# A Hymba-style layer: the gate's adaLN on ScalarE and GpSimd, the S5 scan emitted without delay, u's chunks first, q and k in place

## The chip, the core and the metric

The kernel runs on one core of a Trainium2 chip. The metric is the time of one execution on the device in microseconds. The engines are TensorE (PE, with its weight loads PEld), VectorE (DVE), ScalarE (ACT), GpSimd (POOL) and SyncE (SP). SP issues the DMAs of all large weights, POOL those of the small inputs and of data that goes through DRAM. Each engine takes its instructions in the order of its own queue.

## What is computed

One decoder layer on 256 tokens of width 4096, all in fp32:

```python
mod = silu(c) @ w_ada + b_ada
shift, scale, gate = split(mod, 3)
h = x * (1.0 + scale) + shift
q, k, v, g_lr, z_gla, u_s5, z_s5 = split(h @ w_in)
o_gla = RMSNorm_head(GLA(q, k, v, alpha(g_lr))) * silu(z_gla)   # 4 heads, chunks of 64
y = gelu(S5(u_s5))                # 128 groups of 16 channels, 64 complex states each
y = y * sigmoid(y @ w_glu + b_glu)
o_s5 = y * silu(z_s5)
mixed = concat(o_gla, o_s5) @ w_out
x = layer_norm(2 ** 0.25 * x + gate * mixed, ln_g, ln_b)
```

`w_ada` is 4096 x 12288, `w_in` 4096 x 10256, `w_out` 4096 x 4096, `w_glu` 2048 x 2048. Every weight is read once.

## The kernel before

**Matmuls.** Each weight tile of 512 KB comes into one of six `raw` buffers (`raw`, L81; the buffers are shared by all weights, in the order of SP's queue). `split` (L109) makes two fp32r halves of it: ACT rounds it to `hi` (L114) and DVE takes the rest as `lo` (L115). PE then multiplies hi by hi, hi by lo and lo by hi: 12 matmuls for a tile (L211 for `w_in`, L733 for `w_out`, L587 for `w_glu`). There are three buffers each for `hi` and `lo`.

**adaLN.** c @ w_ada is a product with one row only, so it is not done on PE: the pieces of `w_ada` come as 128 x 1024 tiles, 32 to a piece, and DVE adds tile times silu(c) to `rows` (`ada_sums`, L143: the first step at L151, the other 31 at L153). PE then sums `rows` over the partitions. Eight pieces make shift and scale, each for one block of 512 of the 4096 inputs of `w_in` (`ada_steps`). Four more make the gate (`gate_steps`, L704), which is needed at the end alone; its bias and its result pass through POOL's DMAs (L713, L717).

**Input projection.** The 21 column chunks of `KINDS` are visited in each of 8 blocks of the inputs (`win_plan`); some visits take two blocks at once. Partial sums are kept in SBUF and added by DVE (L222). In the last block (b = 7) a chunk is finished. A zs chunk is then transposed and sent to DRAM through POOL (L231, L232). A u chunk is transposed and copied by 32 small ACT copies into `u4` (`s5_u4`, L416). From the ninth chunk on, steps of the S5 work are emitted behind each chunk with `later(LATE)`, which puts them 60 priority steps back; behind a zg chunk a GLA head follows (`gla_head`). It writes the decayed q and k into a buffer of its own, `qkt` (L607, L634, L636).

**S5.** `s5_inputs` (L424) makes the input of the states, `e`, in 16 blocks. Two scans (`s5_scan`, L468), one for each half of the groups, run over 64 chunks of four tokens: 63 steps each, four small DVE instructions to a step (L475 to L478), each step needing the one before. `s5_outputs` (L520) makes 16 blocks of outputs: the states (L502) need the finished scan of their half, `s5_lags` copies a Toeplitz block with 16 ACT copies (L518), and PE (L548) and ACT (L555) finish y. The first scan is driven from `s5_inputs` (blocks 8 to 15, L438), the second from `s5_outputs` (L536, L543), both at the lowered priority of the work around them.

**Order of the end.** First half of the output projection (`wout(cc, 0)`, the GLA channels) with `s5_outputs` between its tiles, then GLU, then the second half with the residuals (L754 to L758), then the layer norm. Gate steps are emitted between the weight tiles of all these, so many to a tile as `GATE_RATES` says: for the S5 chunks of the last block, its other chunks, the first half, GLU, the second half. A scheduler then orders every engine's queue by these priorities and by when it expects inputs to be ready.

Of the kernel before, what the change touches and what calls it, by code (L numbers as in the profile page):

```python
# [14 lines left out]
AF = mybir.ActivationFunctionType  # L15
ALU = mybir.AluOpType
PSUM = bass.MemoryType.PSUM

P = 128
D = 4096  # L20
SEQ = 256
# [4 lines left out]
DK_SCALE = 256 ** -0.5  # L26
# [10 lines left out]
ADA_LEAD = 1  # L37

RATES = (1.3, 0.85)
GATE_RATES = (1.2, 0.2, 0.7, 0.6, 0.6)  # L40

PAIRED = (6, 7, 7, 7, 7, 8, 7)


KINDS = (
    [("zs", i) for i in range(4)]
    + [("u", i) for i in range(4)]
    + [("qk", 0), ("va", 0), ("vb", 0), ("zg", 0)]
    + [c for h in range(1, 4) for c in (("qk", h), ("v", h), ("zg", h))]
)  # L50
# [7 lines left out]
class Emit:  # L58
# [81 lines left out]
        self.gg = load("gg", [P, DV // P], io["gla_norm_g"])  # L140


    def ada_sums(self, piece):  # L143

        nc = self.nc
        self.rows = rows = self.tmp([P, 1024], "rows")
        for kt in range(32):
            t = self.raw([P, 1024], self.io["ada"][piece, kt])
            c = self.silu_c[:, kt : kt + 1]
            if kt == 0:  # L150
                nc.vector.tensor_scalar(out=rows, in0=t, scalar1=c, scalar2=None, op0=ALU.mult)  # L151
            else:
                nc.vector.scalar_tensor_tensor(out=rows, in0=t, scalar=c, in1=rows, op0=ALU.mult, op1=ALU.add)  # L153
            yield
# [269 lines left out]
    def s5_inputs(self):  # L424

        nc = self.nc
        flat = "p k g h -> p (k g h)"

        e = self.bp.tile([P, 162, 2, 32], F32, tag="b32", name="e")
        self.e, self.bcols = [e[:, 1:65], e[:, 98:162]], e[:, 65:97]  # L430

        nc.gpsimd.memset(e[:, 0:98:97], 0.0)

        self.moved = [e[:, 0:97], e[:, 65:161]]
        scans = [self.s5_scan(0), self.s5_scan(1)]
        self.scans = scans
        nb = NPAIR // NB
        scan = lambda b, n: drive(scans[0], n) if b >= 8 else None  # L438
        loads = {b: self.s5_load(self.io["s5_b"][b]) for b in range(2)}
        prep = lambda b: self.pad_products(self.pad[b % 2], loads.pop(b), self.pw[:, :, :, b * NB : (b + 1) * NB], 1, True)  # L440
        prep(0)
        for b in range(nb):
            pad, w1s = self.pad[b % 2], []
            for n2 in range(NB // 2):
                tps = self.zbank([P, 2, 2, P])
                for m in range(2):
                    for ri in range(2):
                        nc.tensor.transpose(out=tps[:, m, ri], in_=pad[:, 2 * n2 + m, ri].rearrange(flat), identity=self.ident)
                w1s.append(self.tmp([P, 2, 2, P], "w1"))
                nc.scalar.copy(out=w1s[-1], in_=tps)  # L450
                if n2 == 0 and b + 1 < nb:
                    prep(b + 1)
                    if b + 2 < nb:
                        loads[b + 2] = self.s5_load(self.io["s5_b"][b + 2])
                scan(b, 3)
                yield
            eps = self.zbank([P, 2, 64, NB])
            for n in range(NB):
                pr = b * NB + n
# [60 lines left out]
    def s5_outputs(self):  # L520


        nc = self.nc
        nb = NPAIR // NB
        self.y = []
        self.ct_next = None
        self.dd = [self.cp.tile([P, NB, 32], F32, name=f"dd{i}") for i in range(2)]
        for t in self.dd:
            nc.gpsimd.memset(t, 0.0)
        self.s5_prep(0)  # L530
        yield
        nxt = None
        for b in range(-1, nb):
            ys = nxt
            if b < 7:
                drive(self.scans[1], 4)  # L536
            if b + 1 < nb:
                kt, nxt = self.s5_states(b + 1)
            if b + 2 < nb:
                self.s5_prep(b + 2)  # L540
            yield
            if b < 7:
                drive(self.scans[1], 4)  # L543
            if b >= 0:
                o = self.zbank([P, NB, 64])
                for n in range(NB):
                    pr = b * NB + n
                    nc.tensor.matmul(o[:, n], lhsT=self.w0[b % 2][:, n], rhs=self.u4[pr // 16][:, pr % 16, :], start=True, stop=True)  # L548
                nc.vector.tensor_tensor(out=o, in0=o, in1=ys, op=ALU.add)
                if b % 4 == 0:  # L550
                    self.y.append(self.slot([P, 4, SEQ], name="y"))
                yv = self.y[-1][:, b % 4].rearrange("p (j c) -> p j c", j=4)
                for a in range(NB):
                    for j in range(4):
                        nc.scalar.activation(out=yv[32 * a : 32 * a + 32, j], in_=o[32 * j : 32 * j + 32, a], func=AF.Gelu_apprx_tanh)  # L555
# [48 lines left out]
    def gla_head(self, h):  # L604
        nc = self.nc
        v = nc.vector
        qk = self.slot([P, 2, 2, SEQ], name="qkt")  # L607
        q, k = qk[:, 0], qk[:, 1]

        ps = self.xbank([P, 2, SEQ])  # L610
        wg = self.tmp([16, 2, P], "wg")
# [19 lines left out]
                            in1=lv[:, :, c - 1, CH - 1 : CH].broadcast_to([P, 2, c]), op=ALU.add)  # L631
        nc.scalar.activation(out=ds_, in_=ds_, func=AF.Exp, scale=1.0 / TAU)
        nc.scalar.activation(out=x, in_=l, func=AF.Exp, scale=1.0 / TAU)
        v.scalar_tensor_tensor(out=q, in0=self.turned(self.acc["qk"][h], 0), scalar=DK_SCALE, in1=x, op0=ALU.mult, op1=ALU.mult)  # L634
        nc.scalar.activation(out=x, in_=l, func=AF.Exp, scale=-1.0 / TAU)
        v.tensor_tensor(out=k, in0=self.turned(self.acc["qk"][h], 2), in1=x, op=ALU.mult)  # L636

        ap = self.xbank([P, 3, P])
        kv = k.rearrange("p t (c n) -> p t c n", n=CH)
# [33 lines left out]
        o = zg  # L673
# [30 lines left out]
    def gate_steps(self):  # L704

        nc, io = self.nc, self.io
        self.gates = []
        for qd in range(4):
            yield from self.ada_sums(8 + qd)
            gate = self.dp.tile([1, 1024], F32, tag=f"gate{qd}", name=f"gate{qd}")  # L710
            for j in range(2):
                b = self.tmp([1, 512], "gb")
                nc.gpsimd.dma_start(out=b, in_=io["b_ada_g"][:, qd * 1024 + j * 512 : qd * 1024 + j * 512 + 512])  # L713
                ps = self.xbank()
                nc.tensor.matmul(ps[0:1], lhsT=self.ones[:, 0:1], rhs=self.rows[:, 512 * j : 512 * j + 512], start=True, stop=True)
                nc.vector.tensor_tensor(out=b, in0=ps[0:1], in1=b, op=ALU.add)
                nc.gpsimd.dma_start(out=gate[:, 512 * j : 512 * j + 512], in_=b)  # L717
            self.gates.append(gate)
# [274 lines left out]
```

## Time and profile before

| | us |
|---|---|
| median of 3 runs | 1730.19 (1728.96 to 1730.79) |
| the profiled execution | 1725.37 |
| its span, first to last instruction | 1723.6 |
| mean granted clock of TensorE | 0.959 |

The profile is one execution on the hardware. The lines quoted below come from it: busy times, windows cut from the span, waits with what ended them, and groups of instructions as "line engine operation, output <- inputs, shapes, count | busy us, mean ns of one | idle us before it". A granted clock of 1.00 is full speed.

### The profile page before, as it was taken

To read this page: it belongs to the slowest core of one execution; us is meant where nothing else is said; L and a number is where in the kernel's file an instruction comes from. 1 tells how busy PE (TensorE), PEld (TensorE's weight loads), DVE (VectorE), ACT (ScalarE), POOL (GpSimd) and SP (SyncE) were. 2 spreads that over 40 slices of the span, in tenths; PEclk is the share of its full clock that TensorE was granted. 3 is DMA by queue.
4 is the path that set the end of the run, shared out by engine and by line. 5 is a ranking of instruction groups with operands and counts; after the bars stand their busy time and mean duration, and the time that the engine had idled before them with its cause. 6 is when DMAs were issued, how large, how long until landed. Compare 5 with 4: busy or idle time off the path is not lost. (4 is left out here: it accounts for less than half of the span.)

```text
span 1723.6 us, 22261 instructions
## 1 busy us (share of the span) xinstructions
PE 1540.7 (89%) x7548; PEld 1282.8 (74%) x7548; DVE 1457.9 (85%) x2096; ACT 830.2 (48%) x1468; POOL 67.2 (4%) x134
## 2 busy tenths in 40 slices
PE   0689999999999999998988999869973989999995
PEld 0577888888888888877777888657763879977773
DVE  7899889898998999988966699978897468979986
ACT  0345434343343433533587777538732975533330
POOL 1000000000000000000000000000000000010000
PEclk9999999999999999999999999978995999999997
DMA  9999999999999999989965546316890279989982
GB/s 363 348 358 347 352 337 346 337 346 352 334 347 341 338 356 336 339 303 323 325 227 200 166 146 204 118 40 188 300 339 16 74 254 312 332 305 359 337 301 109
DMA packets 138066, 480.64 MB, mean 279 GB/s; under 512 B 17899, under 2 KB 18363, under 8 KB 137691
## 3 DMA queue, kind: packets, MB, share of 16 engines
q1 hardware_dynamic: 130240, 457.85, 74.1%
q0 software_dynamic: 7712, 21.37, 3.9%
q8 instruction: 59, 0.97, 0.2%
q14 instruction: 55, 0.45, 0.1%
HBM read 472.77 MB, written 6.39 MB: 278 GB/s over the span
## 5 line engine op out<-in xcount | busy, mean ns | idle before, releaser
L114 ACT CAST hi<-raw 128x1024 fp32r<-128x1024 f32 (+2 forms) x496 | 506.5, 1025 | 647.3 <-DMA raw<-in_w_in 207.6
L115 DVE TENSOR_TENSOR lo<-raw,hi 128x1024 fp32r<-128x1024 f32 (+2 forms) x496 | 583.4, 1186 | 115.1 <-ACT hi L114 110.5
L211 PE MATMUL mm<-hi,hhi 128*128 128x512 f32 (+2 forms) x1344 | 514.0, 386 | 28.3 <-ACT hi L114 22.1
L211 PE MATMUL mm<-hi,hlo 128*128 128x512 f32 (+2 forms) x1344 | 511.2, 383 | 0.0
L153 DVE SCALAR_TENSOR_TENSOR rows<-raw,silu_c,rows 128x1024 f32<-128x1024 f32 x372 | 476.3, 1280 | 32.2 <-DMA raw<-in_ada 28.9
L211 PE MATMUL mm<-lo,hhi 128*128 128x512 f32 (+2 forms) x1344 | 351.6, 383 | 2.6 <-DVE lo L115 2.5
L211 PEld LDWEIGHTS mm<-hi,hhi 128*128 128x128 f32 x1344 | 254.5, 189 | 81.5 <-ACT hi L114 26.4
L211 PEld LDWEIGHTS mm<-hi,hlo 128*128 128x128 f32 x1344 | 254.8, 190 | 48.0 <-issue 0.2
L211 PEld LDWEIGHTS mm<-lo,hhi 128*128 128x128 f32 x1344 | 245.7, 189 | 51.6 <-DVE lo L115 4.9
L733 PE MATMUL mm<-hi,ohi 128*128 128x512 f32 x512 | 205.2, 402 | 5.1 <-ACT hi L114 5.1
L733 PE MATMUL mm<-hi,olo 128*128 128x512 f32 x512 | 203.2, 397 | 0.6 <-DVE olo L683 0.5
L733 PE MATMUL mm<-lo,ohi 128*128 128x512 f32 x512 | 143.6, 400 | 4.1 <-DVE lo L115 4.0
L733 PEld LDWEIGHTS mm<-hi,ohi 128*128 128x128 f32 x512 | 97.8, 191 | 30.9 <-ACT hi L114 7.9
L733 PEld LDWEIGHTS mm<-lo,ohi 128*128 128x128 f32 x512 | 95.1, 190 | 29.4 <-DVE lo L115 8.7
L733 PEld LDWEIGHTS mm<-hi,olo 128*128 128x128 f32 x512 | 97.8, 191 | 21.6 <-DVE olo L683 1.6
L502 PE MATMUL pz<-e,pad 128*128 128x97 f32 (+1 forms) x256 | 51.6, 369 | 41.9 <-DVE e L478 41.9
L502 PEld LDWEIGHTS pz<-e,pad 128*128 128x128 f32 x256 | 48.5, 257 | 45.4 <-DVE e L478 42.7
L587 PE MATMUL mm<-yhl,hi 128*128 128x256 f32 x512 | 68.5, 288 | 5.0 <-ACT hi L114 5.0
L587 PEld LDWEIGHTS mm<-yhl,hi 128*128 128x128 f32 x512 | 65.4, 196 | 5.3 <-ACT hi L114 5.2
L166 PE MATMUL px<-ones,rows 128*128 128x1 f32 x128 | 16.5, 258 | 53.5 <-DVE rows L153 53.5
L518 ACT COPY w<-px 32x128 f32<-32x128 f32 (+3 forms) x256 | 55.5, 217 | 11.3 <-PE px L515 7.0
L166 PEld LDWEIGHTS px<-ones,rows 128*128 128x128 f32 x128 | 17.2, 209 | 54.2 <-DVE rows L153 53.5
(238 smaller groups left out, 1199.1 us busy)
## 6 DMA issues: line engine op xcount, KB each, us to landing
raw<-in_ada SPq DMA_DIRECT2D x384, 512.0 KB, 5.6
raw<-in_w_in SPq DMA_DIRECT2D x304, 512.0 KB, 5.3
raw<-in_w_out SPq DMA_DIRECT2D x128, 512.0 KB, 5.1
raw<-in_w_glu SPq DMA_DIRECT2D x32, 512.0 KB, 4.9
raw<-in_w_vb SPq DMA_DIRECT2D x16, 272.0 KB, 3.8
x<-in_xT POOLq DMA_DIRECT2D x16, 256.0 KB, 5.0
raw<-in_w_va SPq DMA_DIRECT2D x16, 256.0 KB, 4.3
xo<-in_x_tok POOLq DMA_DIRECT2D x8, 512.0 KB, 6.9
```

The source lines that it names most:

```text
L114: nc.scalar.copy(out=hi, in_=src)
L115: nc.vector.tensor_tensor(out=lo, in0=src, in1=hi.bitcast(F32), op=ALU.subtract)
L153: nc.vector.scalar_tensor_tensor(out=rows, in0=t, scalar=c, in1=rows, op0=ALU.mult, op1=ALU.add)
L166: nc.tensor.matmul(ps[:, s, kt : kt + 1], lhsT=self.rows[:, 512 * s + kt * P : 512 * s + kt * P + P], rhs=self.ones[:, 0:1], start=True, s ...
L211: nc.tensor.matmul(ps[:, m, 0:w], lhsT=t[:, 2 * half + kt, m * P : m * P + P], rhs=r[:, kt], start=st, stop=en)
L502: nc.tensor.matmul(yps[:, n, 0 : moved.shape[1]], lhsT=pad[:, n, ri].rearrange("p k g h -> p (k g h)"), rhs=moved[:, :, ri, (b * NB + n) % ...
L518: nc.scalar.copy(out=w0[32 * j : 32 * j + 32, n, 32 * j : P], in_=kps[32 * n : 32 * n + 32, 0 : P - 32 * j])
L587: nc.tensor.matmul(ps[:, m], lhsT=w[:, kt, m * P : m * P + P], rhs=t[:, kt, :], start=u == 0 and j == 0, stop=u == 3 and j == len(todo) - 1)
L733: nc.tensor.matmul(ps[:, it], lhsT=t[:, 2 * n2 + m, it * P : it * P + P], rhs=w[:, m], start=first and j in (0, 2), stop=last and j >= len ...
```

## The change

- `ada_sums` gets a form `aside`, used for the gate's four pieces: ACT multiplies a tile by silu(c) in place (the first one into `rows`), and POOL adds it to `rows`. DVE has no part in it. A tile's buffer is now free when POOL has read it.
- `GATE_RATES` is 0.85 throughout.
- The scans are emitted with the delay taken back (`later(-LATE)`, `later(-BG_LATE)`), and the second one in sixes.
- In `KINDS` u's four chunks stand ahead of zs's.
- `gla_head` writes q and k into the buffer of their own projection sums, `acc["qk"][h]`, and makes both transposes before the first write.

```diff
-GATE_RATES = (1.2, 0.2, 0.7, 0.6, 0.6)
+GATE_RATES = (0.85, 0.85, 0.85, 0.85, 0.85)
...
-    [("zs", i) for i in range(4)]
-    + [("u", i) for i in range(4)]
+    [("u", i) for i in range(4)]
+    + [("zs", i) for i in range(4)]
...
+            if aside:
+                o = t if kt else rows
+                nc.scalar.activation(out=o, in_=t, func=AF.Copy, scale=c)
+                if kt:
+                    nc.gpsimd.tensor_tensor(out=rows, in0=t, in1=rows, op=ALU.add)
+            elif kt == 0:
...
-        scan = lambda b, n: drive(scans[0], n) if b >= 8 else None
+        def scan(b, n):
+            with self.later(-LATE):
+                drive(scans[0], n if b >= 8 else 0)
...
-            if b < 7:
-                drive(self.scans[1], 4)
+            with self.later(-BG_LATE):
+                drive(self.scans[1], 6)
...
-        qk = self.slot([P, 2, 2, SEQ], name="qkt")
-        q, k = qk[:, 0], qk[:, 1]
+        qk = self.acc["qk"][h]
+        q, k = (qk[:, t].rearrange("p (t n) -> p t n", t=2) for t in range(2))
...
+        tq, tk = (self.turned(qk, t) for t in (0, 2))
...
-            yield from self.ada_sums(8 + qd)
+            yield from self.ada_sums(8 + qd, True)
```

The lines of the changed kernel are up to 10 higher than those of the kernel before: L743 is L733 there, L511 is L502, L557 is L548, L484 to L487 are L475 to L478, L514 is L505; the gate's products are L152, its sums L154.

**PE, ninth block of states.** PE's queue in the first half of the output projection, where it first needs the second scan (`e`); before:

```order
L733 MATMUL mm_11202<-hi_11448,olo_9262 128x512
L733 MATMUL mm_11202<-lo_11449,ohi_9261 128x512 x4
L502 MATMUL pz_10787<-e,pad_391 128x96 x8
L548 MATMUL pz_10827<-u_1339_6912,w_1_394 128x64 x4
L515 MATMUL px_10870<-ident,kt_10796 128x128
L502 MATMUL pz_10912<-e,pad_392 128x96 x8
L515 MATMUL px_11017<-ident,kt_10921 128x128
```

and in the changed kernel:

```order
L743 MATMUL mm_11045<-hi_11239,olo_8606 128x512
L743 MATMUL mm_11045<-lo_11240,ohi_8605 128x512 x4
L511 MATMUL pz_10933<-e,pad_391 128x96 x8
L557 MATMUL pz_10977<-u_1285_6666,w_1_394 128x64 x4
L743 MATMUL mm_11045<-hi_11283,ohi_9371 128x512
```

Before, 576 of the 768 matmuls of this half stand ahead of the ninth block, 280 of them since the eighth, and three blocks follow one another; now 456 stand ahead, 108 since the eighth, and matmuls of the projection stand between the blocks.

**DVE, the second scan.** Two of its late steps on DVE, before (`rows` is the gate's sum):

```order
L115 TENSOR_TENSOR lo_11575<-raw_11572,hi_11574 128x1024
L477 TENSOR_TENSOR sc_1993_9872<-sc_1993_9872,e 128x64
L153 SCALAR_TENSOR_TENSOR rows_9747<-raw_11610,silu_c,rows_9747 128x1024
L478 TENSOR_TENSOR e<-sc_1993_9872,sc_1994_9873 128x64
L475 TENSOR_TENSOR sc_1995_9878<-a_307,e 128x64
L476 TENSOR_TENSOR sc_1996_9879<-a_307,e 128x64
L477 TENSOR_TENSOR sc_1995_9878<-sc_1995_9878,e 128x64
L153 SCALAR_TENSOR_TENSOR rows_9747<-raw_11653,silu_c,rows_9747 128x1024
L478 TENSOR_TENSOR e<-sc_1995_9878,sc_1996_9879 128x64
```

and the scan's last two steps now, with the first use of its result (`kt`):

```order
L115 TENSOR_TENSOR lo_11240<-raw_11237,hi_11239 128x1024
L486 TENSOR_TENSOR sc_2129_10483<-sc_2129_10483,e 128x64
L487 TENSOR_TENSOR e<-sc_2129_10483,sc_2130_10484 128x64
L484 TENSOR_TENSOR sc_2131_10489<-a_307,e 128x64
L485 TENSOR_TENSOR sc_2132_10490<-a_307,e 128x64
L486 TENSOR_TENSOR sc_2131_10489<-sc_2131_10489,e 128x64
L487 TENSOR_TENSOR e<-sc_2131_10489,sc_2132_10490 128x64
L115 TENSOR_TENSOR lo_11284<-raw_11281,hi_11283 128x1024
L514 TENSOR_TENSOR kt_10942<-pz_10933,dd_9440 128x128
```

The gate's steps no longer stand among the scan's. Counted in this stage's splits (L115), the second scan ends behind 51 of them before and behind 38 now; between the ends of the two scans stood 31 gate steps.

**ACT and POOL in GLU.** ACT's queue in GLU before:

```order
L114 CAST hi_12432<-raw_12430 128x1024
L114 CAST hi_12465<-raw_12463 128x1024
L114 CAST hi_12495<-raw_12493 128x1024
L592 ACTIVATE sg_12421<-mm_12291,bglu 128x256 x2
L114 CAST hi_12528<-raw_12526 128x1024
L600 CAST ohi_12425<-sg_12421 128x2x4x64
```

and now (L601 and L609 are L592 and L600):

```order
L152 ACTIVATE raw_12453<-raw_12453,silu_c 128x1024
L114 CAST hi_12459<-raw_12457 128x1024
L152 ACTIVATE raw_12487<-raw_12487,silu_c 128x1024
L114 CAST hi_12503<-raw_12501 128x1024
L601 ACTIVATE sg_12491<-mm_12354,bglu 128x256 x2
L114 CAST hi_12533<-raw_12531 128x1024
L609 CAST ohi_12350<-sg_12491 128x2x4x64
L152 ACTIVATE raw_12561<-raw_12561,silu_c 128x1024
```

A product now stands ahead of most splits. POOL's queue has seldom more than DMA issues before; in GLU it now reads:

```order
L587 DMA zsq_12498<-zsd 128x1024
L154 TENSOR_TENSOR rows_12129<-raw_12419,rows_12129 128x1024
L154 TENSOR_TENSOR rows_12129<-raw_12453,rows_12129 128x1024
L154 TENSOR_TENSOR rows_12129<-raw_12487,rows_12129 128x1024
L154 TENSOR_TENSOR rows_12129<-raw_12561,rows_12129 128x1024
```

Each sum waits for its product and for the sum before it, and SP's load into the buffer waits for the sum. Of the gate's 128 loads in SP's queue, 26 stood in the last block of the input projection, 45 in the first half of the output projection, 19 in GLU and 38 in the second half; now it is 45, 55, 26 and 2.

More of the change, by code (lines that the diff above doesn't have):

```diff
@@ L140, in consts, with ada_sums @@
         self.gg = load("gg", [P, DV // P], io["gla_norm_g"])
-    def ada_sums(self, piece):
+    def ada_sums(self, piece, aside=False):
         nc = self.nc
@@ L149, in ada_sums @@
             c = self.silu_c[:, kt : kt + 1]
-            if kt == 0:
+            if aside:
[4 more added lines that the diff above has]
+            elif kt == 0:
                 nc.vector.tensor_scalar(out=rows, in0=t, scalar1=c, scalar2=None, op0=ALU.mult)
@@ L541, in s5_outputs @@
             yield
-            if b < 7:
-                drive(self.scans[1], 4)
+            with self.later(-BG_LATE):
+                drive(self.scans[1], 6)
             if b >= 0:
@@ L633, in gla_head @@
         nc.scalar.activation(out=x, in_=l, func=AF.Exp, scale=1.0 / TAU)
-        v.scalar_tensor_tensor(out=q, in0=self.turned(self.acc["qk"][h], 0), scalar=DK_SCALE, in1=x, op0=ALU.mult, op1=ALU.mult)
+        tq, tk = (self.turned(qk, t) for t in (0, 2))
+        v.scalar_tensor_tensor(out=q, in0=tq, scalar=DK_SCALE, in1=x, op0=ALU.mult, op1=ALU.mult)
         nc.scalar.activation(out=x, in_=l, func=AF.Exp, scale=-1.0 / TAU)
-        v.tensor_tensor(out=k, in0=self.turned(self.acc["qk"][h], 2), in1=x, op=ALU.mult)
+        v.tensor_tensor(out=k, in0=tk, in1=x, op=ALU.mult)
         ap = self.xbank([P, 3, P])
```

## The prediction

> **What bounds the kernel now.** I read the page's busy shares first, then cut the span into six stages with the windows view, and then asked which waits of TensorE (PE) end last in each stage.
>
> ```profile
> PE 1540.7 (89%) x7548; PEld 1282.8 (74%) x7548; DVE 1457.9 (85%) x2096; ACT 830.2 (48%) x1468; POOL 67.2 (4%) x134
> ```
>
> PE is nearest to full, DVE next, and POOL is almost empty. These are averages. The windows below are P0 (everything up to the last block of the input projection), C (that last block), W0 (first half of the output projection, with the S5 outputs), G (GLU), W1 (second half of the output projection) and the tail T.
>
> ```profile
> 0.00:838.00 838.00, 758.47 (x3511) 631.72 (x3512) 746.59 (x817) 333.77 (x377) 17.86 (x38) 1.00 0.94 341
> 838.00:1075.00 237.00, 226.42 (x1228) 188.88 (x1228) 185.75 (x327) 172.71 (x331) 15.91 (x34) 0.98 0.61 205
> 1075.00:1409.50 334.50, 267.42 (x1246) 219.42 (x1245) 259.31 (x692) 200.86 (x615) 14.28 (x28) 0.86 0.47 158
> 1409.50:1509.90 100.40, 95.36 (x775) 94.91 (x774) 86.76 (x76) 56.32 (x82) 2.65 (x5) 0.97 0.92 330
> 1509.90:1695.00 185.10, 181.11 (x776) 143.33 (x774) 160.12 (x147) 66.16 (x65) 16.50 (x30) 1.00 0.84 303
> 1695.00:1723.60 28.60, 11.96 (x18) 4.56 (x18) 19.33 (x42) 0.36 (x1) 0.00 (x0) 0.55 0.39 147
> ```
>
> Columns: length, then busy time of PE, PE's weight loads, DVE, ACT, POOL, then granted clock, DMA share, GB/s. W1, C and G keep PE at 95 to 98%. P0's loss is mostly one wait of 53.5 us at its start. W0 is the poor stage: 267.4 of 334.5 us, at a clock of 0.86. PE's waits there (us, times, longest), behind that one of P0:
>
> ```profile
> PE px L166 <- DVE rows L153: 53.5, 1, 53.5
> ...
> PE pz L502 <- DVE e L478: 41.9, 2, 34.4
> PE pz L548 <- ACT y L555: 7.0, 3, 3.3
> PE pz L548 <- ACT w L518: 4.9, 8, 1.5
> ```
>
> Two waits make 41.9 us: the S5 states (L502) stand in PE's queue behind the last step of a scan on DVE (L478). Each also costs clock. Four windows of 20 us around them, same columns:
>
> ```profile
> 1140.00:1160.00 20.00, 12.42 (x49) 9.79 (x50) 15.52 (x65) 7.15 (x32) 1.57 (x3) 0.63 0.09 32
> 1160.00:1180.00 20.00, 17.37 (x75) 13.64 (x75) 15.36 (x29) 17.38 (x63) 2.63 (x5) 0.76 0.47 139
> 1300.00:1320.00 20.00, 1.82 (x8) 1.83 (x9) 17.29 (x96) 0.00 (x0) 0.00 (x0) 0.50 0.00 0
> 1320.00:1340.00 20.00, 13.94 (x63) 13.17 (x63) 9.94 (x20) 15.39 (x68) 1.07 (x2) 0.50 0.02 7
> ```
>
> From 1300 to 1320 PE stands and DVE is busy; then PE works 13.94 us at half clock. At full clock those 13.94 would take 7.0, the 12.42 at 0.63 would take 7.8 and the 17.37 at 0.76 would take 13.2: 15.8 us lost, as far as clock scales busy time.
>
> **The change part by part.**
>
> *Scan.* Its 126 steps are the same instructions, only emitted without the delay. The order shows why a wait can go: before, PE asks for the ninth block of states after 576 of W0's 768 matmuls; now after 456, and the scan's end has moved from behind 51 of this stage's splits (L115) to behind 38, which is where PE's 456 matmuls (12 each) stand. Before, 31 of the gate's multiply-adds stood between the two scans' ends too.
>
> ```profile
> L153 DVE SCALAR_TENSOR_TENSOR rows<-raw,silu_c,rows 128x1024 f32<-128x1024 f32 x372 | 476.3, 1280 | 32.2 <-DMA raw<-in_ada 28.9
> L151 DVE TENSOR_SCALAR rows<-raw,silu_c x12: 733/750/755, 10.8 to 1536.3; 128x1024 f32<-128x1024 f32 x12
> ```
>
> 31 times 1.28 is 40 us less in front of the second scan, more than the 34.4 it is late. So I take both waits as gone: 41.9 + 15.8 = 57.7 us gross, and C plus W0 shrink from 571.5 to 513.8. What is late next is below.
>
> *Gate.* DVE loses 124 x 1.280 + 4 x 0.75 = 161.7 us. ACT gains 128 products, POOL 124 sums. The nearest ACT rows:
>
> ```profile
> L114 ACT CAST hi<-raw 128x1024 fp32r<-128x1024 f32 x464 | 486.5, 1052 | 605.0 <-DMA raw<-in_w_in 207.6 <-PE mm L211 161.0 <-DMA raw<-in_w_out 84.6
> L175 ACT ACTIVATE x<-x,m 128x256 f32<-128x256 f32 x32 | 16.6, 591 | 59.0 <-DVE m L170 58.9
> L176 ACT CAST hhi<-x 128x256 fp32r<-128x256 f32 x32 | 10.9, 400 | 0.0
> L416 ACT COPY u<-px 32x128 f32<-32x128 f32 x128 | 32.9, 257 | 3.1 <-PE px L246 1.5
> ```
>
> L175 reads two operands per partition and is 191 ns longer than L176 of the same size; the product reads one, so 1052 + 95 = 1147 ns. By the load order, the gate's loads become 45 in C, 55 in W0, 26 in G, 2 in W1 (26, 45, 19, 38 before). ACT in C and W0 then has 172.71 + 200.86 + 100 x 1.147 = 488.3 us of work, 95% of the 513.8. The densest long stretch that ACT reaches in this trace is 39.43 of 43 us, 92%:
>
> ```profile
> 1333.00:1376.00 43.00, 40.67 (x206) 36.11 (x206) 19.00 (x32) 39.43 (x155) 0.00 (x0) 0.88 0.22 69
> ```
>
> At 91.7% the two stages need 532.5 us. **ACT takes the scan's place as the bound, and 57.7 gross becomes 39.0 net.** PE then runs (226.4 + 267.4 - 15.8) / 532.5 = 90%, and DVE (185.8 + 259.3 less the 71 steps that its loads put there, 91) is at 66%. Behind a product in ACT's queue stand the splits that PE waits for, so this load is on the path.
>
> No row shows a POOL sum. The nearest is a memset of the same tile, one pass over it:
>
> ```profile
> L385 POOL MEMSET pad<- x2: 978/978/978, 3.5 to 4.4; 128x1024 f32 x2
> ```
>
> From below 0.98 us; from above three such passes (two reads, one write), 2.93; I take two, 1.96, as if the write runs beside the reads, and keep both ends. 98 sums in C and W0 are then 192 us (96 to 287) beside 30 of other work in 532: hidden as long as nothing is shared. A sum also holds its load buffer, so the load queue (SP) now waits for POOL, and POOL's own DMA issues (S5 weights, zsd, the next gate's bias) stand between sums. In G one step in 100.4 / 32 = 3.1 us leaves room for 0.85 of a sum at any of the three prices.
>
> The Trainium skill (GPSIMD Engine Reference, Elementwise — side-by-side cycle accounting) gives 4497 ns for an fp32 sum of 2048 elements; half of it, 2.25 us, is an estimate by that page, and no run shown here has such a sum. With it the sum of this part stays as it is.
>
> *G.* Loads rise from 51 to 58 in the order and ACT from 56.3 to 86 of 100.4 us. A DMA share of 0.92 times 58/51 is 1.05, 5 us too much where P0 sustains 0.94, unless some loads land earlier, as W0's share of 0.47 lets them. I cost it at 0 (-2 to +6): its first wait stays ACT's, the first row here:
>
> ```profile
> PE mm L587 <- ACT hi L114: 5.0, 1, 5.0
> PE mm L733 <- DVE lo L115: 2.7, 4, 1.1
> ```
>
> *W1* (second row) loses nearly all gate work, 36 loads and 44.7 us of DVE; PE is at 181.1 of 185.1, so it gains 3 at most; I take 3. *T* has none of it: 0.
>
> *u first.* 32.9 us of ACT copies (L416) move ahead of the zs chunks, but products now stand between them; in C, PE's waits are these:
>
> ```profile
> PE mm L211 <- ACT hi L114: 4.8, 2, 4.4
> PE px L246 <- ACT u L416: 4.5, 3, 2.7
> ```
>
> ACT's total in C is counted above, so I add nothing (-9.3 to +10). *q, k in place* drops four buffers and issues the same instructions; k's transposes must now end before q is written: 0, and at most half of the 4.9 us that they all take. P0 has the same chunk widths: 0.
>
> ```profile
> L246 PE MATMUL px<-ident,qk 128*128 128x128 f32 x32 | 4.9, 274 | 0.0
> ```
>
> **Sum.** The profiled execution took 1725.37 us (span 1723.6 and 1.8 around it); 1725.4 - 39.0 - 3.0 = 1683.4. It lies 4.8 under the median of the three runs, 1730.19, against which the change is timed, so the forecast is 1688.
>
> **The rivals.**
>
> *PE-bound (1656).* ACT packs better than in any long stretch so far, and C and W0 run at C's PE share of 95.5%: 478 / 0.955 = 500.5, 71 saved instead of 39. Against it: the L548 waits on ACT, 11.9 us, exist already with less on ACT.
>
> *POOL and DVE in turn (slower, about 1750).* DVE's instructions with two inputs in SBUF and POOL's sums share something and run one at a time. DVE's work of that kind in G and in C plus W0:
>
> ```profile
> 838.00:1075.00 237.00, 68.55 (x58) 0.98 0.61 205
> 1075.00:1409.50 334.50, 72.29 (x60) 0.86 0.47 158
> 1409.50:1509.90 100.40, 40.80 (x34) 0.97 0.92 330
> L475 DVE TENSOR_TENSOR sc<-a,e 128x64 f32<-128x64 f32 x126 | 28.0, 222 | 2.6
> L477 DVE TENSOR_TENSOR sc<-sc,e 128x64 f32<-128x64 f32 x126 | 27.4, 218 | 0.0
> L396 DVE TENSOR_TENSOR ta<-bc,pw 128x512 f32<-128x512 f32 x32 | 20.8, 685 | 0.0
> L396 DVE TENSOR_TENSOR ta<-bc,af 128x512 f32<-128x512 f32 x32 | 20.5, 677 | 0.0
> L399 DVE TENSOR_TENSOR ta<-ta,ta 128x512 f32<-128x512 f32 x16 | 11.0, 686 | 0.0
> L406 DVE TENSOR_TENSOR pad<-ta,ta 64x512 f32<-64x512 f32 x32 | 21.8, 682 | 1.0 <-PE pz L502 0.7
> L580 DVE TENSOR_TENSOR y<-y,zsq 128x1024 f32<-128x1024 f32 x4 | 8.2, 2043 | 0.0
> L593 DVE TENSOR_TENSOR sg<-y,sg 128x512 f32<-128x512 f32 x8 | 5.5, 685 | 0.0
> L601 DVE TENSOR_TENSOR olo<-sg,ohi 128x512 fp32r<-128x512 f32 x8 | 8.9, 1114 | 0.0
> ```
>
> The first three rows are L115 alone by stage. C plus W0: 140.8 + 4 x 27.7 for the scan + 74.1 = 326; G: 63.4. With a sum of p us, G needs 63.4 + 27p instead of 100.4 and C plus W0 326 + 98p instead of 532.5. Both excesses together eat the 42 us from p = 2.28. At 1.96 this costs 16 in G alone, 1704; at 2.45, midway to the upper end, 29 + 34, which gives 1751; at 2.93, 1811. For it: a scan step is a chain of four such instructions, so its wait would come back. Against it: nothing in this trace, which has no POOL read.
>
> The Trainium skill (SBUF — State Buffer, Who interferes with whom) states this rule: a VectorE instruction with two SBUF inputs and a GpSimd instruction that reads SBUF exclude each other for whole instructions. By it and the 2.25 us above the change would about break even; no run here can show it yet, and the trace neither agrees nor disagrees.
>
> *ACT packs worse (1727).* At 85% busy C and W0 need 574, and only W1's 3 us remain, less G's start.
>
> *The scan's wait half stays (1709).* The change then does only half of what it says: the scan's last steps and PE's request moved up together (38 splits, 456 matmuls), and if DVE's queue is held by the splits' waits for ACT, one of the two waits returns at about half of 42.
>
> **How the numbers follow.** Forecast 0.45, its own range 1670 to 1705; PE-bound 0.13; POOL and DVE in turn 0.27; ACT packs worse 0.08; wait half stays 0.07. From 1652 to 1752 all but the edges of the first rival and the dearer half of the second are in. A measurement of this kernel tells about 0.2%, 3.5 us, from no change. Faster: 0.45 + 0.13 + 0.07 and a little of the second rival, 0.67; within 0.2%: 0.06; slower 0.27.
>
> **What would show it.** PE's wait for L478 gone and the clock of W0 near 0.95: the scan step is right. ACT above 90% through C and W0 with PE waiting for L114 or L518: the bound is right. L115 stretched beyond 1.19 us, or POOL sums stretched where DVE is busy, and G longer than 105 us: the second rival. Sums above 2.3 us would make my forecast wrong even without it, since the load queue waits for them.

## The result and the profile after

| | before | after |
|---|---|---|
| median of the timed runs, us | 1729.58 (1726.97 to 1730.79) | 1839.44 (1834.70 to 1847.42) |
| span of the profiled execution, us | 1723.6 | 1837.2 |
| mean granted clock of TensorE | 0.959 | 0.938 |

The changed kernel is slower: its time is 1.0651 of that before (95% interval 1.0628 to 1.0674), where the forecast said 1688 us and a range up to 1752.

The page after, its row of busy times:

```profile
PE 1598.9 (87%) x7548; PEld 1318.0 (72%) x7548; DVE 1517.1 (83%) x1968; ACT 963.6 (52%) x1596; POOL 398.9 (22%) x258
```

DVE lost 128 gate instructions and yet is busy for 59 us more (1457.9 before). Something stretched those that stayed.

The windows view of the kernel after, by stage. Columns as before: length, busy time of PE, its weight loads, DVE, ACT, POOL, then clock, DMA share, GB/s. C and W0 are taken together, because the edge between them is not sharp in every kernel: from 838 us to the GLU's first matmul.

```profile
0.00:838.00 838.00, 758.75 (x3498) 632.50 (x3498) 740.95 (x807) 336.19 (x378) 22.16 (x39) 0.99 0.93 340
838.00:1497.00 659.00, 545.57 (x2492) 436.23 (x2493) 520.18 (x960) 477.28 (x1050) 270.03 (x155) 0.87 0.53 177
1497.00:1628.70 131.70, 105.80 (x770) 100.98 (x769) 111.71 (x51) 81.89 (x102) 88.06 (x37) 0.92 0.78 271
1628.70:1807.90 179.20, 176.78 (x772) 143.77 (x770) 123.86 (x110) 67.87 (x66) 18.64 (x28) 1.00 0.67 218
```

Cut in the same way, the kernel before has 570.6, 101.3 and 183.9 us in the last three rows. Its row of C and W0:

```profile
838.00:1408.60 570.60, 492.94 (x2465) 407.40 (x2465) 444.15 (x1016) 372.73 (x942) 30.19 (x62) 0.91 0.52 177
```

So C and W0 took 88.4 us more, G 30.4 more, W1 4.7 less: 114.1, against 113.6 between the two spans. DVE is busy for 520 us in C and W0 (444 before) though it has 56 instructions fewer.

The waits of PE in the kernel after (us in total, times, longest):

```profile
PE px L171 <- DVE rows L158: 54.6, 1, 54.6
PE mm L743 <- DVE lo L115: 37.0, 13, 6.1
PE mm L216 <- ACT hi L114: 19.8, 12, 5.4
PE mm L596 <- DVE lo L115: 18.7, 17, 4.0
PE mm L216 <- DVE lo L115: 16.8, 7, 6.7
```

The two waits for the scan, 41.9 us before, are not in the list any more. In their place stand waits for L115, the second half of a split: 37.0 us in W0 and W1 (4.0 before), 18.7 in G (none before) and 16.8 in the input projection (2.5 before). The groups of instructions behind that, in the kernel after (of the first row busy us and mean ns, of the others ns least/median/most):

```profile
L115 DVE TENSOR_TENSOR lo<-raw,hi 128x1024 fp32r<-128x1024 f32 (+2 forms) x496 | 666.8, 1356 | 173.3 <-ACT hi L114 167.9
L487 DVE TENSOR_TENSOR e<-sc,sc x126: 205/224/2535, 1020.5 to 1370.1; 128x64 f32<-128x64 f32 x126
L152 ACT ACTIVATE raw<-raw,silu_c x124: 1131/1149/1185, 830.8 to 1623.2; 128x1024 f32<-128x1024 f32 x124
L154 POOL TENSOR_TENSOR rows<-raw,rows x124: 2342/2467/3622, 832.0 to 1634.0; 128x1024 f32<-128x1024 f32 x124
```

L115 grew from 583.4 to 666.8 us, and the scan's last step, never far from its 0.22 us before, takes up to 2.5. The product on ACT is at the 1.147 us of the forecast; the sum on POOL is at 2.34 to 3.62 instead of 1.96. The timeline of DVE shows what the long steps are:

```profile
1077.51 2.54 DVE L487 TENSOR_TENSOR e<-sc,sc 128x64 f32<-128x64 f32 x1
1080.08 2.38 DVE L484 TENSOR_TENSOR sc<-a,e 128x64 f32<-128x64 f32 x1
1082.38 0.21 DVE L485 TENSOR_TENSOR sc<-a,e 128x64 f32<-128x64 f32 x1
```

and in the same timeline the engine POOL (x2 are two sums behind each other):

```profile
1077.58 4.80 POOL L154 TENSOR_TENSOR rows<-raw,rows 128x1024 f32<-128x1024 f32 x2
```

Two sums run from 1077.58 to 1082.38. Two instructions of the scan, of 0.22 us else, take 2.54 and 2.38 us beside them and end when they end, and the third, at 1082.38, is short again. DVE gets one instruction through for each sum. It is so in the whole trace: all 31 scan instructions that took over 0.32 us end 0.08 to 0.09 us after a sum does, and all 49 splits of 128x1024 over 1.32 us end 1.08 to 1.09 us after one.

### The profile page after: what moved, and what is told of

The parts are those of the page before. It is cut to its first block, busy times and chain, and to the rows that moved or that the text cites. A ratio compares the mean times of both kernels' runs of the same rounds, so it can differ in the third digit from the quotient of the medians.

```text
span 1837.2 us, 22440 instructions
## 1 busy us (share of the span) xinstructions
PE 1598.9 (87%) x7548; PEld 1318.0 (72%) x7548; DVE 1517.1 (83%) x1968; ACT 963.6 (52%) x1596; POOL 398.9 (22%) x258
## 4 chain that ended last, share of the span: by engine, by line
PE 51%; DVE 20%; ACT 14%; issue 7%; DMA 7%; SPq 0%; DVEq 0%; ACTq 0%
PE mm L216 36%; PE mm L743 11%; DVE lo L115 6%; ACT hi L114 3%; DVE rows L158 3%; DMA raw<-in_ada 3%; ACT w L527 2%; ACT y L564 2%; ACT raw L152 2%; DMA raw<-in_w_in 2%; DVE e L487 2%; ACT u L421 2%; DVE sc L484 2%; DMA raw<-in_w_glu 1%; PE mm L596 1%
## 5 line engine op out<-in xcount | busy, mean ns | idle before, releaser
L115 DVE TENSOR_TENSOR lo<-raw,hi 128x1024 fp32r<-128x1024 f32 (+2 forms) x496 | 666.8, 1356 | 173.3 <-ACT hi L114 167.9
L216 PE MATMUL mm<-hi,hhi 128*128 128x512 f32 (+2 forms) x1344 | 522.0, 391 | 25.7 <-ACT hi L114 19.8
L216 PE MATMUL mm<-hi,hlo 128*128 128x512 f32 (+2 forms) x1344 | 518.9, 389 | 2.0 <-DVE hlo L182 2.0
L154 POOL TENSOR_TENSOR rows<-raw,rows 128x1024 f32<-128x1024 f32 x124 | 333.2, 2687 | 345.5 <-ACT raw L152 324.6
L216 PE MATMUL mm<-lo,hhi 128*128 128x512 f32 (+2 forms) x1344 | 356.9, 388 | 17.3 <-DVE lo L115 16.8
L158 DVE SCALAR_TENSOR_TENSOR rows<-raw,silu_c,rows 128x1024 f32<-128x1024 f32 x248 | 317.7, 1281 | 19.3 <-DMA raw<-in_ada 16.3
L743 PE MATMUL mm<-hi,ohi 128*128 128x512 f32 x512 | 211.7, 414 | 13.1 <-ACT hi L114 11.6
L743 PE MATMUL mm<-hi,olo 128*128 128x512 f32 x512 | 210.2, 411 | 4.6 <-DVE olo L693 4.6
L743 PE MATMUL mm<-lo,ohi 128*128 128x512 f32 x512 | 153.1, 418 | 37.0 <-DVE lo L115 37.0
L152 ACT ACTIVATE raw<-raw,silu_c 128x1024 f32<-128x1024 f32 x124 | 141.9, 1149 | 70.1 <-DMA raw<-in_ada 63.4
L743 PEld LDWEIGHTS mm<-lo,ohi 128*128 128x128 f32 x512 | 100.6, 200 | 63.9 <-DVE lo L115 42.6
L743 PEld LDWEIGHTS mm<-hi,ohi 128*128 128x128 f32 x512 | 101.1, 198 | 39.9 <-ACT hi L114 16.0
L166 POOL DMA_DIRECT2D x<-in_xT x16 | 8.8, 551 | 535.2 <-DVE hlo L182 458.0
L743 PEld LDWEIGHTS mm<-hi,olo 128*128 128x128 f32 x512 | 100.6, 197 | 27.7 <-DVE olo L693 7.2
L564 ACT ACTIVATE y<-pz 32x64 f32<-32x64 f32 x256 | 55.1, 215 | 16.2 <-DVE pz L558 13.3
```

Of the source, the lines that this page charges most:

```text
L115: nc.vector.tensor_tensor(out=lo, in0=src, in1=hi.bitcast(F32), op=ALU.subtract)
L152: nc.scalar.activation(out=o, in_=t, func=AF.Copy, scale=c)
L154: nc.gpsimd.tensor_tensor(out=rows, in0=t, in1=rows, op=ALU.add)
L216: nc.tensor.matmul(ps[:, m, 0:w], lhsT=t[:, 2 * half + kt, m * P : m * P + P], rhs=r[:, kt], start=st, stop=en)
L743: nc.tensor.matmul(ps[:, it], lhsT=t[:, 2 * n2 + m, it * P : it * P + P], rhs=w[:, m], start=first and j in (0, 2), stop=last and j >= len ...
```

## The experiments

Edits are shown against the changed kernel, or against the kernel before where that is said. Ratios are to the kernel before.

### Is it POOL's reading?

**pool_writes**

```
-  nc.gpsimd.tensor_tensor(out=rows, in0=t, in1=rows, op=ALU.add)
+  nc.gpsimd.memset(t, 0.0)
+  nc.gpsimd.memset(t, 0.0)
+  nc.gpsimd.memset(t[:, 0:512], 0.0)
```

> The changed kernel with each POOL sum replaced by POOL memsets of the same load buffer, one and a half tiles more than one pass (2.5 x 0.98 us, about the 2.34 us of an undisturbed sum). The gate's sums are left out, so the output is not the reference's. POOL is as busy, each load buffer is held as long and POOL's queue is the same, but POOL reads nothing. Theory 1, DVE instructions with two SBUF inputs and POOL's reads shut each other out: L115 is back at 1.19 us mean (1.36 in the changed kernel), the scan's lines at 0.22, and the time falls by 100 or more, to 1670 to 1720. Theory 2, load buffers held longer by the slower engine and POOL's DMA issues behind the sums starve the stream: it stays at 1800 or more. Theory 3, the products in ACT's queue hold up the splits: it stays at 1800 or more as well.

1739.46 us, 1.0065 (1.0042 to 1.0088). The groups of this kernel:

```profile
L115 DVE TENSOR_TENSOR lo<-raw,hi 128x1024 fp32r<-128x1024 f32 (+2 forms) x496 | 584.6, 1188 | 256.8 <-ACT hi L114 245.5
L489 DVE TENSOR_TENSOR e<-sc,sc x126: 197/224/472, 1034.0 to 1319.1; 128x64 f32<-128x64 f32 x126
```

L115 and the scan are back at their times of before, with POOL as long at work for each step (2.4 us), the same loads, buffers and products. So 100 of the 110 us lost go with the sums themselves, and not with the time for which POOL is busy or holds a load buffer. But the forecast's gain isn't there either, and the 1670 to 1720 us expected of this run are missed:

```profile
838.00:1430.40 592.40, 525.05 (x2491) 423.82 (x2490) 377.12 (x954) 472.63 (x1051) 256.48 (x347) 0.92 0.59 199
```

C and W0 still take 592.4 us, 22 more than before, with ACT 80% busy and DVE 64%. That is taken up below.

**pool_reads**

```
-  nc.gpsimd.tensor_tensor(out=rows, in0=t, in1=rows, op=ALU.add)
+  nc.gpsimd.tensor_scalar(out=t, in0=t, scalar1=1.0, scalar2=None, op0=ALU.mult)
+  nc.gpsimd.tensor_scalar(out=t, in0=t, scalar1=1.0, scalar2=None, op0=ALU.mult)
```

> The changed kernel with each POOL sum replaced by two POOL instructions that read the load buffer and write it back (times 1.0), one input each; the gate's sums are left out, so the output is not the reference's. Theory 1 in the form that POOL's reads shut out DVE's second input: L115 is stretched again (mean above 1.25 us; 1.188 with memsets, 1.356 in the changed kernel) and the time is 1770 to 1850, against 1739 with memsets of the same count of elements. If only a POOL instruction with two inputs does it: L115 at 1.19 and 1730 to 1750.

2147.16 us, 1.2416 (1.2377 to 1.2455), and most of that because the two passes of a step take 5.5 us, where a sum takes 2.5:

```profile
L154 POOL TENSOR_SCALAR raw<-raw x124: 2758/2769/4057, 833.6 to 1941.7; 128x1024 f32<-128x1024 f32 x124
L115 DVE TENSOR_TENSOR lo<-raw,hi 128x1024 fp32r<-128x1024 f32 (+2 forms) x496 | 593.8, 1204 | 562.2 <-ACT hi L114 558.1
```

POOL holds the load buffers, and PE waits for splits whose loads come late. So the time, above both ranges that were expected, says nothing of DVE. DVE is stretched less than beside the sums, but it is stretched: 1204 ns a split against 1356 (1186 before), and 143.1 us for the scan's four lines against 176.1 (110.9 before). The timeline, POOL and DVE rows of two places:

```profile
1118.09 2.78 POOL L155 TENSOR_SCALAR raw<-raw 128x1024 f32<-128x1024 f32 x1
1118.13 1.08 DVE L488 TENSOR_TENSOR e<-sc,sc 128x64 f32<-128x64 f32 x1
1119.25 0.22 DVE L485 TENSOR_TENSOR sc<-a,e 128x64 f32<-128x64 f32 x1
...
1499.66 1.27 DVE L402 TENSOR_TENSOR ta<-bc,af 128x512 f32<-128x512 f32 x2
1499.88 3.70 POOL L155 TENSOR_SCALAR raw<-raw 128x1024 f32<-128x1024 f32 x1
...
1501.57 1.35 DVE L115 TENSOR_TENSOR lo<-raw,hi 128x1024 fp32r<-128x1024 f32 x1 [0.64 <-ACT hi L114]
```

In the first place a scan instruction that begins beside the POOL pass takes 1.08 us instead of 0.22, and the next one is short again while the same pass goes on. In the second place L115 starts 1.69 us behind the pass's start and ends inside it. The whole trace has one pattern: of the 40 scan instructions that took over 0.32 us beside such a pass, 36 end 1.64 to 1.66 us before a pass ends, and all nine splits of 128x1024 over 1.32 us end 0.64 to 0.66 us before. So a pass that reads one input shuts DVE out too, but only for about its first 1.1 us of 2.77, where the sum does so to its end. The mean of the splits, by which this run was to decide, hides that. It goes the other way as well: the 160 passes that began while DVE had no instruction with two SBUF inputs at work took at most 0.05 us over the least; the other 88, like the one of 3.70 us that begins beside L402, took 0.27 us over it in the mean.

**sum_dve, gate_dve, aside_only.** The products on ACT and the sums on DVE; the gate wholly back on DVE; and, against the kernel before, the gate's move and the new rates without the rest.

```
sum_dve:     nc.gpsimd.tensor_tensor(...)  ->  nc.vector.tensor_tensor(...)
gate_dve:    self.ada_sums(8 + qd, True)   ->  self.ada_sums(8 + qd)
aside_only:  before + ada_sums(8 + qd, True) + GATE_RATES = (0.85, 0.85, 0.85, 0.85, 0.85)
```

> The changed kernel with products on ACT as changed and the sums on DVE (one TENSOR_TENSOR of 1.22 us for each, where before there was one of 1.28). POOL reads nothing. Theory 1: 1690 to 1740, with no stretched DVE line. Theory 2: 1700 to 1760, since buffers are free sooner. Theory 3 (ACT's products are the loss): 1800 or more.

> The changed kernel with the gate's adaLN on DVE as before (one instruction per tile), all other parts kept, rates 0.85. Theories 1 to 3, which all blame the gate's move: 1680 to 1725, the scan's wait of 41.9 us smaller than half. A theory 4, that the scan's new place, u first or q and k in place make the loss: 1800 or more.

> The kernel before with only the gate's adaLN moved to ACT and POOL, and rates 0.85. Theory 1: 1830 to 1880, as in the changed kernel or worse, for the late scan is stretched too and its end is awaited by PE; theory 4: 1730 to 1760.

1768.37 us (1.0231, 1.0204 to 1.0258), 1755.70 (1.0164, 1.0135 to 1.0193) and 1856.47 (1.0737, 1.0712 to 1.0762). Without POOL's sums the loss is 39 and 26 us of the 110, between the ranges that were expected of either run; with the gate's move and the rates alone it is all there and 17 us more. But gate_dve, with no work on another engine, ought to have been near the kernel before and isn't. PE's waits in it:

```profile
PE pz L511 <- DVE e L487: 37.0, 2, 27.5
PE px L689 <- DVE zg L681: 28.2, 2, 18.7
```

The scan's two waits are back, and a third place waits 28.2 us for DVE, where it was 6.0. What is left of the change in this kernel is the scan's new place, the rates, the order of chunks, and q and k.

### The scan's place and the rates

All three against the kernel before, but for the last, which is the changed kernel with the gate on DVE and the old rates.

```
scan_only:
-  scan = lambda b, n: drive(scans[0], n) if b >= 8 else None
+  def scan(b, n):
+      with self.later(-LATE):
+          drive(scans[0], n if b >= 8 else 0)
...
-  if b < 7:
-      drive(self.scans[1], 4)
+  with self.later(-BG_LATE):
+      drive(self.scans[1], 6)
rates_only:      GATE_RATES = (0.85, 0.85, 0.85, 0.85, 0.85)
gate_dve_rates:  ada_sums(8 + qd), GATE_RATES = (1.2, 0.2, 0.7, 0.6, 0.6)
```

> The kernel before with only the scan's emission changed (both scans without delay, the second in sixes). If the scan's place was the cause of the two waits of 41.9 us, as the prediction took it: 1670 to 1700. If the scan ends when DVE's total work lets it and only displaces other DVE work that PE needs (the GLA heads' norm, L671): 1725 to 1760, with a longer PE wait for L671.

> The kernel before with only the rates at 0.85. More of the gate's steps then stand on DVE in the last projection block, the first half and GLU, fewer in the second half. If the rates make the 26 us that the changed kernel with the gate on DVE is over the kernel before: 1745 to 1765. If the scan's place or u first make them: 1720 to 1735.

> The changed kernel with the gate on DVE and the rates of before: so scan, u first, and q and k in place alone. If the rates make the 26 us: 1690 to 1730. If the scan's place or u first make them: 1745 to 1765.

scan_only: 1728.40 us, 0.9993 (0.9979 to 1.0007). The edit does nothing there: on PE, DVE, POOL and the load queue the instructions stand in the very order of before, on ACT one split moves. gate_dve_rates: 1731.16, 1.0008 (0.9994 to 1.0021); the scan, the chunks' order and q and k come to nothing together. rates_only: 1764.66, 1.0200 (1.0178 to 1.0221): with the gate on DVE, the even rates alone cost 35 us. PE's waits in it:

```profile
PE pz L502 <- DVE e L478: 39.7, 2, 26.8
PE px L679 <- DVE zg L671: 26.8, 2, 18.3
```

### Where the expected gain went

Four kernels take the parts off one by one. gate_late is the kernel before with no gate step ahead of the GLU; the other three are pool_writes or the changed kernel with the old rates.

```
gate_late:         before, GATE_RATES = (0, 0, 0, 0.85, 1.4)
writes_old_rates:  pool_writes, GATE_RATES = (1.2, 0.2, 0.7, 0.6, 0.6)
aside_old_rates:   after, GATE_RATES = (1.2, 0.2, 0.7, 0.6, 0.6)
no_products:       writes_old_rates, and
-  o = t if kt else rows
-  nc.scalar.activation(out=o, in_=t, func=AF.Copy, scale=c)
-  if kt:
+  if kt == 0:
+      nc.scalar.activation(out=rows, in_=t, func=AF.Copy, scale=c)
+  else:
```

> The kernel before with one edit: the gate's sums, still on VectorE, all go out from the GLU on (rates 0, 0, 0, 0.85, 1.4), so that C and W0 hold none of them and ScalarE gets nothing more. It is a look at the most that the forecast's gain could be. The forecast's reading (the gate's VectorE work is what makes the scan late): both waits of TensorE for the scan go, and C plus W0 come from 571.5 us to 510 to 520. The rival (the scan's own chain and the short hand-overs bound the stage, the gate's instructions only fill what would be idle): the two waits keep at least half of their 76 us, and C plus W0 stay at 545 or more. In both, G and W1 get longer by what VectorE cannot do beside TensorE there, so the total says little: 1700 to 1760 us.

> The kernel with writes in place of the sums, and the rates of before (1.2, 0.2, 0.7, 0.6, 0.6) in place of 0.85. If the rates are what kept that kernel's C plus W0 at 592 us (42 products in C where the old rates put about 28), C plus W0 come to 545 to 565 us and the total to 1695 to 1715. If it is ScalarE's products as such, wherever they stand, C plus W0 stay within 10 us of 592 and the total at 1730 to 1745.

> The changed kernel with the rates of before in place of 0.85. POOL's sums still shut VectorE out of its own SBUF reads, so the time stays well above before: 1800 to 1835 us if the rates cost what they cost with the gate on VectorE (some 25 to 35 us), 1835 to 1850 if the number of sums beside VectorE is all that counts. Below 1760 would speak against the exclusion as the main cause.

> The kernel with writes for sums and the old rates, with the gate's products left out as well, but the first of each piece (124 of 128): the loads and POOL's writes stay. Its sums are left out too. C plus W0 of the kernel before take 571 us, with the gate held back to the GLU 525, with products, writes and the old rates 558. If ScalarE's 1.15 us products are what takes back those 33 us, C plus W0 fall to 525 to 535 here and the time to 1690 to 1705. If it is the loads of the gate's rows or their buffers, C plus W0 stay at 550 to 562 and the time at 1715 to 1728.

(The 76 us in the expectation of gate_late are 41.9: its longest wait, 34.4 us, is in that total already.)

Windows of gate_late, C with W0, then G, then W1:

```profile
838.00:1363.30 525.30, 487.59 (x2468) 409.22 (x2468) 369.33 (x949) 376.02 (x956) 26.45 (x54) 0.94 0.41 131
1363.30:1462.90 99.60, 95.36 (x771) 94.95 (x771) 90.03 (x80) 52.32 (x72) 2.64 (x5) 0.97 0.93 332
1462.90:1714.00 251.10, 205.69 (x780) 149.43 (x779) 232.72 (x207) 66.83 (x65) 18.55 (x33) 0.94 0.97 358
```

Without the gate on DVE, and with nothing put on ACT, C and W0 fall by 45.3 us. Most of the gain that the forecast saw there exists, and the waits for the scan fall to 11.2 us. Of no_products and of writes_old_rates the same first window:

```profile
838.00:1361.30 523.30, 483.88 (x2465) 400.21 (x2465) 369.98 (x950) 375.80 (x954) 188.20 (x259) 0.95 0.58 197
```

```profile
838.00:1396.40 558.40, 501.04 (x2456) 410.98 (x2455) 368.52 (x949) 440.94 (x1017) 185.96 (x257) 0.92 0.54 184
```

no_products has the gate's loads and POOL's writes and still is at 523.3: loads and buffers cost nothing while ACT has no part in these steps. The products bring it to 558.4: with 65.1 us of work more on ACT the stage is 35.1 longer, although ACT is busy for only 79% of it. About half of the 35.1 is PE longer at work (483.88 to 501.04 us, at a clock of 0.95 and then 0.92), half is PE standing (39.4 to 57.4 us). PE's waits in C and W0 of writes_old_rates:

```profile
PE pz L559 <- ACT y L566: 11.1, 6, 3.3
PE pz L513 <- DVE e L489: 10.2, 2, 9.6
PE px L253 <- ACT u L423: 7.5, 4, 2.6
PE mm L745 <- ACT hi L114: 7.3, 5, 3.5
PE px L691 <- DVE zg L683: 6.4, 1, 6.4
```

The scan's wait is a quarter of what it was before the change, as in no_products (11.9), and four rows of short waits stand beside it, none over 6.4 us at once and most for ACT. Three of them are in no_products too, at 8.2 (L559), 6.0 (L253) and 6.3 us (L745). ACT itself waits in the same stretch of writes_old_rates:

```profile
ACT raw L152 <- DMA raw<-in_ada: 44.1, 27, 5.2
```

For 44.1 us ACT stood before a product whose tile had not landed, and whatever followed in its queue, splits among it, stood with it. So the 35.1 us are the price of 65.1 us of work and of these waits together; no run tells the two apart. All stages together (us; "writes" are pool_writes' memsets in the place of the sums):

| kernel | the gate in C and W0 | C and W0 | G | W1 | time |
|---|---|---|---|---|---|
| before | on DVE | 570.6 | 101.3 | 183.9 | 1729.6 |
| gate_late | none | 525.3 | 99.6 | 251.1 | 1760.5 |
| no_products | loads and writes, old rates | 523.3 | 101.6 | 181.6 | 1678.2 |
| writes_old_rates | products, writes, old rates | 558.4 | 106.1 | 184.0 | 1724.5 |
| pool_writes | products, writes, new rates | 592.4 | 99.2 | 178.1 | 1739.5 |
| aside_old_rates | products, sums, old rates | 615.1 | 108.0 | 202.7 | 1798.2 |
| after | products, sums, new rates | 659.0 | 131.7 | 179.2 | 1839.4 |

writes_old_rates has ratio 0.9974 (0.9953 to 0.9994), aside_old_rates 1.0405 (1.0372 to 1.0439), gate_late 1.0184 (1.0147 to 1.0221) and no_products 0.9706 (0.9686 to 0.9726). Even if POOL's sums disturbed nothing, the move would be worth 0.3% at the old rates. Of these four, writes_old_rates (expected 1695 to 1715) came out dearer than expected, aside_old_rates and no_products cheaper, and the C and W0 of gate_late lies between its two expectations.

### Can the gain be had?

Four settings of the kernel before's own rates (1.2, 0.2, 0.7, 0.6, 0.6), gate on DVE:

```
late_some:   1.2, 0.2, 0.45, 0.8, 0.8
late_more:   1.2, 0.2, 0.25, 0.9, 1.0
early_some:  1.2, 0.6, 0.4, 0.6, 0.6
early_more:  1.2, 1.0, 0.15, 0.6, 0.6
```

> The kernel before with only other rates (1.2, 0.2, 0.45, 0.8, 0.8 for 1.2, 0.2, 0.7, 0.6, 0.6): some 13 of W0's 38 sums on VectorE stand in the GLU and W1 instead. If the gate's VectorE work in the scan's stretches is what costs, C plus W0 fall by 8 to 14 us (46 us for the 64 sums that the kernel with all of them late took out) and W1 takes up to 5 us of it back: 1718 to 1726. If W1 is already full on VectorE there, each of the 8 or so sums added to it costs its 1.28 us and the time stays at 1726 to 1734.

> As the run before with rates 1.2, 0.2, 0.25, 0.9, 1.0: some 25 of W0's 38 sums stand in the GLU and W1. C plus W0 fall by 15 to 25 us; W1 gets 10 to 20 sums more, of which VectorE's 25 idle us in W1 hold about 19: 1706 to 1722 if they go in there, 1728 to 1745 if they come on top of W1.

> The kernel before with only other rates (1.2, 0.6, 0.4, 0.6, 0.6 for 1.2, 0.2, 0.7, 0.6, 0.6): some 15 of W0's 38 sums on VectorE stand in C instead, where VectorE is 51 us idle. If it is VectorE's share of W0 that makes the scan late, the waits for e L478 shrink by 15 us or more, C plus W0 fall from 571 us by 5 to 15 and the time to 1715 to 1725. If the sums in C stand before the scan's first half as well and hold it up by their own time, C plus W0 stay within 5 us and the time at 1725 to 1735.

> As the run before with rates 1.2, 1.0, 0.15, 0.6, 0.6: some 30 of W0's 38 sums stand in C. If room in C is what counts, 1700 to 1718; if they hold up the scan's first half and the GLA's products in C, 1730 to 1760, with VectorE over 90% busy in C.

1731.63 us (1.0015, 1.0000 to 1.0030), 1731.34 (1.0016, 1.0001 to 1.0031), 1745.35 (1.0100, 1.0080 to 1.0120), 1734.81 (1.0057, 1.0038 to 1.0076). None beats the kernel before. Windows of late_more, C with W0 and then W1:

```profile
838.00:1385.90 547.90, 489.93 (x2468) 409.52 (x2467) 414.49 (x990) 376.30 (x955) 28.48 (x58) 0.93 0.49 164
...
1486.20:1698.50 212.30, 190.05 (x776) 141.08 (x774) 187.47 (x171) 67.90 (x66) 16.69 (x30) 1.00 0.89 323
```

It holds 40 gate steps in C and W0 instead of 64 and gains 22.7 us there; W1 holds 57 instead of 35 and is 28.4 longer, 1.29 us for each of the 22, which is DVE's time for one, as if W1 had no free room on DVE (the dearer expectation). ACT's wait there for loads of the output weights rose from 68.3 to 105.1 us as well, so DVE and the loads are not told apart in W1. In early_more the C window alone reads:

```profile
838.00:1075.00 237.00, 218.87 (x1161) 182.44 (x1159) 196.80 (x270) 156.72 (x304) 17.53 (x34) 0.96 0.73 254
```

PE did 226.42 us there before. The scan's waits are almost gone in that kernel (7.1 us), but those for zg (L671) and q (L636) come instead, 12.2 and 8.8 us: the head's own work now stands behind the gate. early_some lies above both of its expectations: its C and W0 take 586.5 us, with 31.2 us of waits for the scan and 15.4 for zg; why it is dearer than early_more is open. No order of the gate on DVE was found that pays.

## Why the prediction was wrong, point by point

The sum by its terms, in C and W0, from the table (last column added up: 88.4 us, as the two profiles have it):

| term | forecast | measured | from |
|---|---|---|---|
| DVE cleared of the gate: waits and clock | -57.7 | -47.3 | before to no_products |
| products on ACT | +18.7 | +35.1 | no_products to writes_old_rates |
| the even rates (more steps in C and W0) | in the row above | +34.0 | writes_old_rates to pool_writes |
| POOL's sums | 0 | +66.6 | pool_writes to after |

The last two rows depend on their order: at the old rates the sums cost 56.7 us, and with the sums the rates cost 43.9. They depend on the cut too, since 838 us is not the same point of the work in every kernel. Counted from the matmul with which C begins in the kernel before (the 3376th of the input projection), the four rows are -44.5, +37.7, +24.7 and +63.9.

- **"Hidden as long as nothing is shared" is the step that failed.** It made POOL's term zero, and it was the largest: 66.6 us in C and W0, and G's 30.4 with it, since G is at 99.2 us with writes in place of sums. The rival "POOL and DVE in turn" named the mechanism, and in G its size too: 63.4 + 27p at the measured median p of 2.467 is 130.0, measured 131.7 (29 sums began there, not 27, so the near hit has some luck in it). In C and W0 it said 326 + 98p, 568, and 659 came: it started from a stage that ACT held at 532.5, where pool_writes without the sums needs 592.4, and it let the two engines fill each other's gaps without loss. The range cut its dearer half off by the price of 1.96, taken from a memset, which has no input.
- **The Trainium skill (SBUF — State Buffer, Who interferes with whom)** had the rule that decided: two SBUF inputs on VectorE against a read by GpSimd, for whole instructions. The sums agree with it: 2.54 us for an instruction of 0.22 us, which ends with the sum. The passes with one input agree in part: they shut DVE out, but for about 1.1 us of their 2.77 and not to their end, and there the measurement decides. The Trainium skill (GPSIMD Engine Reference, Elementwise — side-by-side cycle accounting) led to an estimate of 2.25 us for a sum; the least here is 2.34. That sentence was nearer than the memset.
- **The scan's waits go, as forecast, but not by the scan's edit.** The edit moves one split on ACT in the kernel before. The shift that the forecast read in the order (the scan's end behind 38 splits instead of 51) is not its work either: with the edit the end stands behind 51 again in gate_dve, sum_dve, no_products, writes_old_rates and aside_old_rates, and behind 43 in pool_writes; without it, behind 51 in gate_late and 48 in aside_only. It moves only where the gate is off DVE and the rates are even. At 51, with the gate late or off DVE, the waits for the scan are 10.2 to 11.9 us; where the end has moved, none to 1.1. So most of the 41.9 us goes by the forecast's other reason, the 40 us of gate steps that leave DVE's queue ahead of the second scan. All the gate's steps together are worth 45 to 47 us of C and W0, against 57.7. Of the 47.3, PE stands 38.2 us less and works 9.1 us less, at a clock of 0.95 instead of 0.91; the forecast had 41.9 and 15.8 for these two.
- **"ACT takes the scan's place as the bound": the direction was right, the size was not.** ACT's work was well counted, 488.3 us against 472.6 in pool_writes. The 91.7% busy share was not reached: 80% there, 79% in writes_old_rates. The forecast counted the products' work and not their waits: with those for the gate's loads (52.1 and 44.1 us) ACT is taken for 89% and 87% of the stage. The best 43 us of the trace, which held no product, was no measure for 590. With 80% the forecast's own working gives 488.3 / 0.80 = 610, slower than before even with harmless sums. That is the rival "ACT packs worse", whose 85% was still too good. (Its own sum leaves 1730 us, not 1727: 574 us is 3 over 571.5, which takes up W1's 3.)
- **The rates** entered the forecast only as a count of loads. With the gate on DVE they cost 35 us by themselves, and with products and writes 25 to 34 in C and W0, by the cut, of which G and W1 gave about 13 back; the two times are 15 us apart.
- **W1** gained 4.7 us, 3 were forecast. The product's 1.147 us came out at 1.149. **u first, q and k in place** were costed at 0; at the old rates with the gate on DVE they and the scan's edit come to 0 together. With the sums in place, the three took 17 us off (aside_only to after); which of them, no run tells.

## What to carry to other kernels

Before work is moved to an idle engine, ask which engine it can shut out while it runs, and price the victims: 124 sums cost DVE 83 us in L115 and 65 in the scan (110.9 to 176.1 us over its four lines), and the shortest instructions suffer most for their size, since each can wait for a whole sum. An engine that hands pieces to two others in turn did not fill up here to the best share it ever reached: take the share of the stage, not that of its best stretch, and count what the new instructions will wait for at the head of its queue. And when a change has several parts, look at the order of each part alone before one of them is given the credit.

## What the runs showed of the hardware, unexpected

On POOL a pass with one input and one output over 128x1024 f32 (TENSOR_SCALAR, 2.77 us at the median in its less disturbed line) is dearer than the sum of two such tiles (2.34 at least, 2.47 at the median); a memset of it takes 0.96. The dearer one disturbs DVE less: 1204 ns a split against 1356, though POOL was at it for 709 us (349.9 and 358.9) and at the sums for 333. By where the stretched DVE instructions end, the sum holds DVE's instructions with two SBUF inputs off to its end, the pass with one input for about its first 1.1 us, and beside a memset they are as short as without one (splits of 128x1024 that began beside one 1.225 us at the median, the others 1.219). Why the pass lets go early is not shown.
